# A hybrid diffusion step: the second chunk's operand forms made between products, and the squares of the group norm made during the attention

## Chip, core and metric

The kernel runs as one program on one core of a Trainium2 chip. The metric is the device time of one execution in microseconds, taken as the median of several runs. Engines are named as in the profile: TensorE (PE), VectorE (DVE), ScalarE (ACT), GpSimd (POOL) and SyncE (SP, which issues nearly all DMAs). In the trace each engine runs its own instructions in one fixed order, so one that waits holds up those behind it.

## What is computed

The reference is one inference step of a two-layer trunk over 1024 latent and 256 context tokens of width 1024. Cut to what matters here, a layer is:

```python
y = jnp.concatenate([rmsnorm(y_hy, gg[:D_HYENA]),
                     rmsnorm(y_sc, gg[D_HYENA:D_HYENA + D_SCONV]),
                     rmsnorm(y_at, gg[D_HYENA + D_SCONV:])], axis=-1)
x = x + g1 * (y @ P['w_out'][l])

h2 = rmsnorm(x, P['g_norm2'][l]) * (1 + sc2) + sh2
ff = (jax.nn.silu(h2 @ P['w_ff_gate'][l]) * (h2 @ P['w_ff_up'][l])) @ P['w_ff_down'][l]
x = x + g2 * ff
```

Three mixers (a long convolution, a short one and an attention of 8 heads) give `y_hy` (256 channels), `y_sc` (256) and `y_at` (512). Each group has its own RMS norm, and one output projection follows. Then comes a gated feed-forward part of inner width 2816. All is float32.

## The kernel before

**Layout.** Channels lie on the 128 partitions and tokens along the free dimension. Tokens are cut into three chunks (`CH`): 0 and 1 are 512 latent tokens each, 2 is the 256 context tokens. A float32 product is made of three matmuls: each operand is split into a high part (a cast on ScalarE) and a low part (a subtraction on VectorE or GpSimd), and high·high, high·low and low·high are added up in PSUM (`mm3`, `mma`; matmul lines L354 and L362). Such a pair of high and low is called a form.

**Order.** The program is written once; a planner then sets the order on each engine, mostly that of the program, with later work put into gaps that it foresees. A second planner lays out the memory called the arena: a buffer may lie where an earlier one was, and then its first write waits for the earlier one's last reader. `self.al` takes a buffer from the arena; rings (`t5`, `hb`, `sw`, `raw`) are small sets of slots used in turn.

**Attention and norm of groups.** `mla` runs blocks (head, bi), bi 0 being the context, 1 and 2 the latent halves, ending with (6,0) (6,1) (7,0) (7,1) (6,2) (7,2). In a block each turn makes one tile of scores (PE, tile `st`), its exponentials (ACT, L1292, tiles `pt`), a running sum of them (POOL, L1295) and every other turn the products with the values (PE, L1277). Some turns after a block of an odd head, `divide` adds up the sums (PE, L1316), takes the reciprocal (DVE, L1325) and multiplies (POOL, L1326). After the division of head 7, `tail` calls `group_norm` for chunk 2, 0 or 1. This loads seven stored tiles of that chunk (`yd`, two DMAs, L1445 and L1446; the eighth tile is the last head pair's result), squares all eight (ACT, L500 and L503) and adds the squares in groups of 2, 2 and 4 (DVE, L504). `bcast_rstd` sums over partitions (PE, L526), takes the inverse root in eleven small steps on DVE (L376 to L383), makes a diagonal (DVE, L535) and broadcasts it (PE, L539). Then each tile is scaled (DVE, L1457) and split (ACT L1459, DVE or POOL L1460). The output projection of chunk 2 runs as a filler inside the attention with one pair of weight buffers (`zo`); that of chunks 0 and 1 comes behind it with weights in `zw`. Its results are added to x (DVE, L1479).

**Gate and up.** The 22 tiles of the inner width are taken in 11 sets j of two, each for `w_gate` (g) and `w_up` (u). The latent product of a set is a 2×2 by 2×2 block product with seven products in place of eight: A is the weight (two inner tiles, two halves of the 1024 inputs), B the tokens (two halves of the inputs, chunks 0 and 1). Weight forms beside the blocks are S1 = A21+A22, S2 = S1−A11, S3 = A11−A21, S4 = A12−S2 (sums on POOL, L1521; high part ACT L1528, low part DVE L1529, in a ring `zq` of five). Token forms are 11 and 21 (chunk 0), 22 (chunk 1's lower half), T1 = B12−B11, T2 = B22−T1, T3 = B22−B12 and T4, which is B21−T2 up to sign. The products are 11·11, 12·21, S2·T2, S1·T1, S3·T3, S4·22 and 22·T4, 12 matmuls of 512 columns each; the context tokens have two plain products of 24 matmuls of 256 columns each (`context`, `contexts`). A set is thus 2 × 132 = 264 matmuls.

Only in set 0 must the token forms of chunk 1 still be made. `rest` does that: `norm2(1)` scales chunk 1 (DVE, L579, eight operations) and `forms_rest` makes the forms, group by group: T2 (POOL L621, DVE L622, cast L614 and subtraction L615, DVE L625), then T1 (L614, L615) with T3's sums (DVE L630), T3's splits, 22 (`shifted`, ACT L594, DVE L595), T4's splits. In the program all of it stands before set 0's first product:

```python
            if j == 0:
                need(0, "g")
                rest()
                first(0, "g")
                first(0, "u")
                for w in "gu":
                    contexts(0, w)
                    free(0, w, "22")
                second(0, "g")
                second(0, "u")
```

`need` fills the free slots of `zq` with weight forms in the order of the list `order`; `first` makes 11·11, one context product and 12·21, `contexts` the other context product, `second` the other five. Results go through `result` (PSUM read by DVE at L1576, L1581, L1585, L1615 and L1623; POOL L1582 multiplies gate and up) into slots of the ring `hb` and from there to memory.

Of the kernel before, what the change touches and what calls it, by code (L numbers as in the profile page):

```python
# [17 lines left out]
P = 128  # L18
# [217 lines left out]
class K:  # L236
# [365 lines left out]
    def forms_rest(self, l, u1, u2):  # L602

        nc = self.nc
        v, gp = nc.vector, nc.gpsimd
        sh = self.mod[l].v(2)[:, 24:32, 0]
        sm = self.small.alloc(4)
        d = sm.f[:, 0:4]
        v.tensor_tensor(out=d, in0=sh[:, 4:8], in1=sh[:, 0:4], op=ALU.subtract)
        F = {n: [None] * 4 for n in ("22", "T1", "T2", "T3", "T4")}  # L610
# [25 lines left out]
        for k in range(4):  # L636
            split("T4", k, u1[4 + k], gp)
        sm.free()
        return F

# [687 lines left out]
    def mla(self, l, tail):  # L1328
# [51 lines left out]
        def divide(head, bi):  # L1380
# [4 lines left out]
            if head == NH - 1:  # L1385
                tail((2, 0, 1)[bi], yats[NG - 1])
# [3 lines left out]
        turn, pend = 0, []  # L1390
        for head, bi in order:
# [48 lines left out]
    def group_norm(self, l, ci, yat):  # L1440
# [5 lines left out]
        nc.sync.dma_start(yv[:, 4:7, :], self.yd[l][:, 4:7, s:s + n])  # L1446
        src = [yv[:, k, :] for k in range(7)] + [yat.f[:, s:s + n]]
        hi, lo = [self.ar(n) for _ in range(KD)], [self.ar(n) for _ in range(KD)]
        groups = ((0, 2), (2, 4), (4, 8))
        accs = [(self.sumsq(src[a:b], n), 1.0 / (P * (b - a))) for a, b in groups]  # L1450
# [43 lines left out]
    def gate_up(self, l, cx, F, rest, extra, ahead):  # L1494
# [8 lines left out]
        order += [(0, w, n) for w in "gu" for n in ("S2", "S1", "S3", "22", "S4")]  # L1503
# [20 lines left out]
        def prepare():  # L1524
# [10 lines left out]
            if n == names[-1]:  # L1535
# [65 lines left out]
        def contexts(j, w):  # L1601
# [3 lines left out]
            result(w, "c", state[w]["E"])  # L1605

        def second(j, w):
# [16 lines left out]
            if j:  # L1624
                contexts(j, w)
# [13 lines left out]

        load(0, "g")  # L1640
        load(0, "u")
        for j in range(NF // 2):
            state["hid"] = {}
            if j == 0:
                need(0, "g")
                rest()
# [5 lines left out]
                second(0, "g")  # L1652
                second(0, "u")
# [76 lines left out]
    def run(self):  # L1730
# [60 lines left out]
        for l in range(DEPTH):  # L1791
# [6 lines left out]
            def tail(n, yat):  # L1798
                y[n] = self.group_norm(l, n, yat)
# [77 lines left out]
            self.close_rings("sw", "hb")  # L1877
# [171 lines left out]
```

## Time and profile before

| | us |
|---|---|
| median of 3 runs | 3706.76 |
| lowest, highest | 3701.41, 3712.45 |
| the profiled execution | 3703.83 |
| its span, first to last instruction | 3701.8 |
| busy in it: PE, DVE, ACT, POOL | 3435.0, 2337.1, 1245.1, 1440.2 |

The profile is of one execution. Its span is 2 us shorter than that execution's own time, and this lies 2.9 us under the median of the runs. Layer 0's gate and up starts near 1040 us, layer 1's near 2808 us; the ends of the two attentions lie around 800 to 940 and 2590 to 2720. In rows of a timeline a number in square brackets is the time that the engine stood idle before the instruction, with what ended that wait.

### The profile page before, as it was taken

What the parts mean: (1) busy time and instruction counts of PE and PEld (TensorE: products, weight loads), DVE (VectorE), ACT (ScalarE), POOL (GpSimd) and SP (SyncE); (2) the same over time, 40 slices, a digit from 0 to 9 for tenths busy, and PEclk for the clock granted to TensorE, in tenths of its full rate; (3) what the DMA queues carried; (4) which work ended last, traced back from release to release, by engine and by line L of the source; (5) the groups of instructions that cost most, each with busy time, mean ns of one, the idle gap of its engine ahead of it and who ended that gap; (6) DMA issues with size and microseconds to landing.
All of it is one profiled execution on the core that took longest, in us unless ns stands there. A gap on an engine that the chain in (4) does not pass through costs nothing.

```text
span 3701.8 us, 45689 instructions
## 1 busy us (share of the span) xinstructions
PE 3435.0 (93%) x17264; PEld 2705.9 (73%) x17264; DVE 2337.1 (63%) x3478; ACT 1245.1 (34%) x2245; POOL 1440.2 (39%) x1097
## 2 busy tenths in 40 slices
PE   7799889997879999999998988999897999999999
PEld 4488865655758888888886886655575888888888
DVE  4657577765476777546667757777658433435666
ACT  3522345544332222221114224555433322222110
POOL 3402346664443333332223223666645323223221
PEclk9899989999989999999999999999898999999999
DMA  7611100013423434342212210000451222214221
GB/s 275 241 60 61 42 10 11 19 39 128 145 65 113 134 123 125 114 154 85 96 58 74 65 47 14 4 11 19 134 165 55 83 69 69 71 61 154 97 77 69
DMA packets 118888, 317.87 MB, mean 86 GB/s; under 512 B 11371, under 2 KB 33387, under 8 KB 112652
## 3 DMA queue, kind: packets, MB, share of 16 engines
q1 hardware_dynamic: 118668, 314.96, 25.7%
q8 instruction: 135, 2.21, 0.3%
q14 instruction: 85, 0.70, 0.1%
HBM read 247.22 MB, written 67.70 MB: 85 GB/s over the span
## 4 chain that ended last, share of the span: by engine, by line
PE 76%; DVE 13%; issue 2%; ACT 2%; POOL 1%; DMA 1%; SPq 0%; DVEq 0%; POOLq 0%; ACTq 0%
PE pb L354 18%; PE pb L362 17%; PE pa L354 14%; PE pa L362 11%; PE st L354 6%; PE y L1277 4%; PE pa L1219 2%; DVE arena L852 1%; DVE arena L853 1%; PE pa L539 1%; PE pa L1238 1%; DVE arena L381 1%; PE pa L1231 1%; PE pa L1221 1%; DVE arena L383 1%
## 5 line engine op out<-in xcount | busy, mean ns | idle before, releaser
L354 PE MATMUL pb<-operands,zw 128*128 128x512 f32 (+1 forms) x2520 | 513.0, 361 | 5.7 <-DVE zw L345 3.0
L354 PEld LDWEIGHTS pb<-operands,zw 128*128 128x128 f32 x2520 | 427.1, 190 | 79.2 <-DVE zw L345 4.9
L362 PE MATMUL pb<-operands,zq 128*128 128x512 f32 (+1 forms) x2467 | 472.5, 348 | 5.5 <-DVE zq L1529 5.5
L1521 POOL TENSOR_TENSOR arena<-arena 128x512 f32<-128x512 f32 x176 | 262.1, 1491 | 523.3 <-DVE zq L1529 506.4
L1528 ACT CAST zq<-arena 128x512 fp32r<-128x512 f32 x356 | 220.8, 621 | 670.0 <-PE pb L362 428.4
L362 PEld LDWEIGHTS pb<-operands,zq 128*128 128x128 f32 x2467 | 391.7, 191 | 70.0 <-DVE zq L1529 6.9
L1529 DVE TENSOR_TENSOR zq<-arena,zq 128x512 fp32r<-128x512 f32 x356 | 288.7, 816 | 181.8 <-ACT zq L1528 177.6
L1295 POOL TENSOR_TENSOR arena<-pt,arena 128x512 f32<-128x512 f32 x256 | 334.7, 1307 | 93.7 <-ACT pt L1292 80.8
L354 PE MATMUL pa<-operands,zw 128*128 128x512 f32 (+1 forms) x1704 | 359.8, 368 | 1.1 <-DVE arena L558 0.6
L354 PEld LDWEIGHTS pa<-operands,zw 128*128 128x128 f32 x1704 | 296.2, 192 | 57.6 <-issue 3.6
L354 PE MATMUL st<-operands 97*128 97x512 f32 (+1 forms) x1056 | 321.0, 409 | 11.1 <-ACT pt L1292 11.1
L362 PE MATMUL pa<-operands,zq 128*128 128x256 f32 (+1 forms) x1801 | 320.8, 334 | 4.2 <-DVE zq L1529 4.2
L362 PEld LDWEIGHTS pa<-operands,zq 128*128 128x128 f32 x1801 | 272.5, 190 | 43.4 <-DVE zq L1529 4.9
L1708 DVE SCALAR_TENSOR_TENSOR arena<-pb,arena 128x512 f32<-128x512 f32 (+1 forms) x330 | 216.4, 661 | 115.4 <-PE pb L354 115.4
L1292 ACT ACTIVATE pt<-st 128x512 f32<-128x512 f32 (+1 forms) x352 | 202.4, 578 | 224.0 <-PE st L354 208.9
L354 PEld LDWEIGHTS st<-operands 97*128 97x128 f32 x1056 | 189.8, 196 | 116.0 <-issue 73.1
L344 ACT CAST zw<-arena 128x1024 fp32r<-128x1024 f32 x102 | 106.5, 1047 | 445.6 <-PE pb L354 374.4
L1277 PE MATMUL y<-pt,kv 128*64 128x512 f32 (+1 forms) x704 | 192.0, 616 | 0.0
L1220 DVE TENSOR_REDUCE arena<-pa 128x1 f32<-128x512 f32 x256 | 168.1, 686 | 34.8 <-PE pa L1219 30.7
L1708 DVE SCALAR_TENSOR_TENSOR arena<-pa,arena 128x512 f32<-128x512 f32 (+1 forms) x198 | 130.9, 661 | 92.8 <-PE pa L354 92.3
L362 PE MATMUL pb<-zf,zq 128*128 128x512 f32 x661 | 175.4, 403 | 10.5 <-DVE arena L1615 10.5
L354 PE MATMUL pb<-ze,zw 128*128 128x512 f32 (+1 forms) x900 | 182.4, 357 | 0.0
(279 smaller groups left out, 5576.6 us busy)
## 6 DMA issues: line engine op xcount, KB each, us to landing
hd<-arena SPq DMA_DIRECT2D x110, 256.0 KB, 2.1
zm<-in_w_modk SPq DMA_DIRECT2D x24, 1024.0 KB, 6.1
arena<-in_w_out SPq DMA_DIRECT2D x48, 512.0 KB, 3.6
arena<-in_w_mod SPq DMA_DIRECT2D x48, 512.0 KB, 3.5
arena<-in_w_g SPq DMA_DIRECT2D x44, 512.0 KB, 3.6
arena<-in_w_u SPq DMA_DIRECT2D x44, 512.0 KB, 3.6
arena<-in_w_dn SPq DMA_DIRECT2D x44, 512.0 KB, 3.8
arena<-hd SPq DMA_DIRECT2D x12, 1280.0 KB, 5.5
```

The source lines that it names most:

```text
L344: nc.scalar.copy(hi.r, raw.f)
L354: self.nc.tensor.matmul(out, a, b, start=(j == 0), stop=(j == n - 1))
L362: self.nc.tensor.matmul(out, a, b, start=(j == 0 and not add), stop=(j == n - 1), skip_group_check=add)
L1219: nc.tensor.matmul(p, q, kh[:96, 512 * c:512 * c + 512], start=True, stop=True)
L1220: v.reduce_max(out=mx[:, t, c:c + 1], in_=p, axis=AX.X)
L1277: ins = nc.tensor.matmul(y[64 * e:64 * e + 64, :n], G["kv"][:, kt0 + k + e, h, 0:64], pts[k + e].f[:, :n], start=(k == 0), stop=(k == nkt ...
L1292: ex = nc.scalar.activation(pt.f[:, :n], st[:, :n], AF.Exp)
L1295: (v if k in KDV else gp).tensor_tensor(out=acc.f[:, :n], in0=pt.f[:, :n], in1=(acc if k > 1 else pts[0]).f[:, :n], op=ALU.add)
L1521: gp.tensor_tensor(out=S[n].f, in0=a, in1=b, op=op)
L1528: nc.scalar.copy(f.r[:, 0:512], src)
L1529: v.tensor_tensor(out=f.r[:, 512:1024], in0=src, in1=f.f[:, 0:512], op=ALU.subtract)
L1708: nc.vector.scalar_tensor_tensor(out=xx, in0=p[:, :n], scalar=g2[:, m, q:q + 1], in1=xx, op0=ALU.mult, op1=ALU.add)
```

## The change

`forms_rest` becomes a generator that stops after each group of forms: T2, then T1, T3 (sums and splits together), 22, T4. Two of T2's four low parts (k = 0 and 2) go from GpSimd to VectorE. The new function `third` replaces `second` for set 0: it takes gate and up together through each product and lets the next group of forms be made behind it. The list of weight forms for set 0 runs in the same pairs, with S4 before 22. The context result c is written later. The ring `hb` has nine slots in place of eight, eight of them cut from the tiles of chunk 0, which therefore are freed at the end of the stage.

`group_norm` is split. `group_sums` allocates the place for the seven stored tiles, loads them, squares them and adds them up (ScalarE and GpSimd, in three buffers of the arena in place of slots of `t5`). It is called before blocks (7,0) and (7,1) for chunks 2 and 0, and in the first turn of block (7,2) for chunk 1. `group_norm` then squares the eighth tile alone and adds it on VectorE.

```diff
-    def forms_rest(self, l, u1, u2):
+    def forms_rest(self, l, u1, u2, F):
...
-            split("T2", k, t2.f, gp)
+            split("T2", k, t2.f, gp if k % 2 else v)
             v.scalar_tensor_tensor(out=u1[4 + k], in0=u1[4 + k], scalar=sh[:, 4 + k:5 + k], in1=t2.f, op0=ALU.add,
                                    op1=ALU.subtract)
             t2.free()
+        yield
         for k in range(4):
             split("T1", k, u1[k], v)
+        yield
+        for k in range(4):
             v.scalar_tensor_tensor(out=u2[k], in0=u2[4 + k], scalar=d[:, k:k + 1], in1=u2[k], op0=ALU.add,
                                    op1=ALU.subtract)
-        for k in range(4):
             split("T3", k, u2[k], gp)
+        yield
         for k in range(4):
             F["22"][k] = self.shifted(l, 4 + k, u2[4 + k])
+        sm.free()
+        yield
         for k in range(4):
             split("T4", k, u1[4 + k], gp)
-        sm.free()
-        return F
+        yield
...
+            if head == NH - 1 and bi < 2:
+                sums[bi] = self.group_sums(l, (2, 0)[bi])
...
+                if (head, bi, k) == (NH - 1, 2, 0):
+                    sums[bi] = self.group_sums(l, 1)
...
-    def group_norm(self, l, ci, yat):
+    def group_sums(self, l, ci):
+
         nc = self.nc
         s, n = CH[ci]
         yr = self.al(7 * n)
...
+        accs = []
+        for a, b in ((0, 2), (2, 4), (4, 7)):
+            acc = self.al(n)
+            nc.scalar.activation(acc.f, yv[:, a, :], AF.Square)
+            for k in range(a + 1, b):
+                q = self.t5(n)
+                nc.scalar.activation(q.f, yv[:, k, :], AF.Square)
+                nc.gpsimd.tensor_tensor(out=acc.f, in0=acc.f, in1=q.f, op=ALU.add)
+                q.free()
+            accs.append(acc)
+        return yr, yv, accs
+
+    def group_norm(self, l, ci, yat, early):
...
+        q = self.t5(n)
+        nc.scalar.activation(q.f, src[7], AF.Square)
+        nc.vector.tensor_tensor(out=accs[2].f, in0=accs[2].f, in1=q.f, op=ALU.add)
...
-        order += [(0, w, n) for w in "gu" for n in ("S2", "S1", "S3", "22", "S4")]
+        order += [(0, w, n) for n in ("S2", "S1", "S3", "S4", "22") for w in "gu"]
...
-            result(w, "c", state[w]["E"])
+            if j:
+                result(w, "c", state[w]["E"])
...
+        def third(more):
+
+            for w in "gu":
+                st = state[w]
+                st["Y"], st["a"] = self.ps(), self.t5()
+                (f,) = need(0, w, "S2")
+                self.mma(st["Y"], ops(f, F["T2"]), False)
+                free(0, w, "S2")
+                v.tensor_tensor(out=st["a"].f, in0=st["Y"], in1=st["p1"].f, op=ALU.add)
+            next(more)
+            for w in "gu":
+                result(w, "c", state[w]["E"])
+            for w in "gu":
+                st = state[w]
+                st["Z"] = self.ps()
+                (f,) = need(0, w, "S1")
+                self.mma(st["Z"], ops(f, F["T1"]), False)
+                free(0, w, "S1")
+            next(more)
...
             if j == 0:
                 need(0, "g")
-                rest()
+                more = rest()
+                next(more)
                 first(0, "g")
                 first(0, "u")
                 for w in "gu":
                     contexts(0, w)
                     free(0, w, "22")
-                second(0, "g")
-                second(0, "u")
+                third(more)
...
             def rest():
                 norm2(1)
-                F.update(self.forms_rest(l, h2[0], h2[1]))
-                x[0].free()
+                self.open_rings(hb0=("f", 512, 1))
+                hb0 = self.rings["hb0"]
+                self.rings["hb"] = Ring(hb0.bufs + Fixed(x[0].f, 4096).cut(512), 512)
+                more = self.forms_rest(l, h2[0], h2[1], F)
+                next(more)
+                yield
+                for _ in more:
+                    yield
                 x[1].free()
-                self.open_rings(hb=("f", 512, 8))
+                yield
```

The part of `third` left out goes on in the same way: S3·T3 and result 22, the next group; S4·22 and result 12, the next group; 22·T4 and result 21.

## Rows read from the trace of the kernel before

**Rows 1.** The page, part 1: busy time, share of the span, instructions of each engine.

```profile
PE 3435.0 (93%) x17264; PEld 2705.9 (73%) x17264; DVE 2337.1 (63%) x3478; ACT 1245.1 (34%) x2245; POOL 1440.2 (39%) x1097
```

**Rows 2.** Waits of PE: line waited for, us in total, times, longest.

```profile
PE pa L362 <- ACT zq L1528: 24.3, 4, 8.9
...
PE pa L526 <- DVE arena L504: 20.5, 9, 6.8
```

**Rows 3.** Windows, L362 alone: PE and PEld busy (matmuls), granted clock, DMA share, GB/s.

```profile
1039.80:1115.60 75.80, 57.00 (x263) 46.09 (x263) 0.84 0.24 77
2808.20:2884.40 76.20, 56.99 (x264) 46.05 (x265) 0.84 0.20 63
...
2900.00:2960.00 60.00, 60.00 (x318) 51.12 (x318) 1.00 0.21 67
```

**Rows 4.** Timeline of PE in layer 0, start of gate and up.

```profile
1064.58 0.40 PE L362 MATMUL pa<-operands,zq 128*128 128x256 f32 x2
...
1083.66 5.06 PE L362 MATMUL pa<-operands,zq 128*128 128x256 f32 x22 [4.15 <-DVE zq L1529]
```

**Rows 5.** Timelines of ACT (first row) and DVE in the same stretch.

```profile
1054.94 0.61 ACT L1528 CAST zq<-arena 128x512 fp32r<-128x512 f32 x1
...
1051.63 5.35 DVE L579 SCALAR_TENSOR_TENSOR arena<-arena,pa 128x512 f32<-128x512 f32 x8 [1.15 <-PE pa L539]
1056.90 2.01 DVE L622 SCALAR_TENSOR_TENSOR arena<-arena 128x512 f32<-128x512 f32 x2
...
1068.63 1.75 DVE L630 SCALAR_TENSOR_TENSOR arena<-arena 128x512 f32<-128x512 f32 x1
...
1082.93 1.88 DVE L1529 TENSOR_TENSOR zq<-arena,zq 128x512 fp32r<-128x512 f32 x3
```

**Rows 6.** POOL's timeline there; L1529's durations in ns, least, median, most.

```profile
1069.80 3.38 POOL L615 TENSOR_TENSOR operands<-arena,operands 128x512 fp32r<-128x512 f32 x2
...
L1529 DVE TENSOR_TENSOR zq<-arena,zq x356: 674/684/1804, 1040.7 to 3376.2; 128x512 fp32r<-128x512 f32 x178
```

**Rows 7.** Timeline of PE in layer 0, end of the attention.

```profile
868.77 1.05 PE L526 MATMUL pa<-arena 128*128 128x1 f32 x8 [2.91 <-DVE arena L504]
...
909.38 5.63 PE L354 MATMUL pb<-operands,zw 128*128 128x512 f32 x24
921.84 1.87 PE L526 MATMUL pa<-arena 128*128 128x1 f32 x8 [6.83 <-DVE arena L504]
...
933.35 5.46 PE L539 MATMUL pa<-arena 128*128 128x512 f32 x6 [3.40 <-DVE arena L535]
```

**Rows 8.** Chain that ended last, two pieces; SP's timeline, the load before.

```profile
913.54 1.30 POOL arena L1326
914.85 5.03 DMA arena<-yd
...
882.01 0.38 SPq L1446 DMA_DIRECT2D arena<-yd  x1
```

**Rows 9.** Timeline of DVE: first root step and first scaling of chunk 1, layer 0.

```profile
930.19 0.17 DVE L376 TENSOR_SCALAR arena<-arena 128x12 int32<-128x12 int32 x1
...
936.04 2.72 DVE L1457 SCALAR_TENSOR_TENSOR arena<-arena,pa 128x512 f32<-128x512 f32 x4
```

**Rows 10.** Timeline of PE in layer 1: first and last of three waits for L504.

```profile
2608.01 1.01 PE L526 MATMUL pa<-arena 128*128 128x1 f32 x4 [2.36 <-DVE arena L504]
...
2700.68 1.05 PE L526 MATMUL pa<-arena 128*128 128x1 f32 x8 [1.21 <-DVE arena L504]
```

**Rows 11.** Window with PE, PEld, DVE, ACT, POOL busy; a wait of ACT; L1295's durations.

```profile
820.00:840.00 20.00, 17.01 (x57) 8.31 (x57) 15.33 (x31) 9.43 (x21) 12.73 (x13) 0.83 0.17 58
...
ACT pt L1292 <- POOL arena L1295: 8.0, 7, 1.3
...
L1295 POOL TENSOR_TENSOR arena<-pt,pt x48: 721/1279/1712, 491.9 to 2644.9; 128x512 f32<-128x512 f32 x32, 128x256 f32<-128x256 f32 x16
```

More of the change, by code (lines that the diff above doesn't have):

```diff
@@ L609, in forms_rest @@
         v.tensor_tensor(out=d, in0=sh[:, 4:8], in1=sh[:, 0:4], op=ALU.subtract)
-        F = {n: [None] * 4 for n in ("22", "T1", "T2", "T3", "T4")}
+        F.update({n: [None] * 4 for n in ("22", "T1", "T2", "T3", "T4")})
         def split(name, k, t, e):
@@ L1385, in divide @@
             if head == NH - 1:
-                tail((2, 0, 1)[bi], yats[NG - 1])
+                tail((2, 0, 1)[bi], yats[NG - 1], sums.pop(bi))
         order = [(head, bi) for head in range(NH - 2) for bi in range(3)]
         order += [(NH - 2, 0), (NH - 2, 1), (NH - 1, 0), (NH - 1, 1), (NH - 2, 2), (NH - 1, 2)]
-        turn, pend = 0, []
+        turn, pend, sums = 0, [], {}
         for head, bi in order:
@@ L1446, in group_norm @@
         nc.sync.dma_start(yv[:, 4:7, :], self.yd[l][:, 4:7, s:s + n])
+        accs = []
[10 more added lines that the diff above has]
+    def group_norm(self, l, ci, yat, early):
+        nc = self.nc
+        s, n = CH[ci]
+        yr, yv, accs = early
         src = [yv[:, k, :] for k in range(7)] + [yat.f[:, s:s + n]]
+        q = self.t5(n)
+        nc.scalar.activation(q.f, src[7], AF.Square)
+        nc.vector.tensor_tensor(out=accs[2].f, in0=accs[2].f, in1=q.f, op=ALU.add)
+        q.free()
         hi, lo = [self.ar(n) for _ in range(KD)], [self.ar(n) for _ in range(KD)]
         groups = ((0, 2), (2, 4), (4, 8))
-        accs = [(self.sumsq(src[a:b], n), 1.0 / (P * (b - a))) for a, b in groups]
+        accs = [(acc, 1.0 / (P * (b - a))) for acc, (a, b) in zip(accs, groups)]
         rs = self.bcast_rstd(accs, n)
@@ L1534, in prepare @@
                     S[m].free()
-            if n == names[-1]:
+            if not any(t[:2] == (j, w) for t in todo):
                 for r in fs:
@@ L1638, in second @@
             p1.free()
+        def third(more):
[16 more added lines that the diff above has]
+            next(more)
+            for w in "gu":
+                st = state[w]
+                (f,) = need(0, w, "S3")
+                self.mma(st["Y"], ops(f, F["T3"]), True)
+                free(0, w, "S3")
+                b = self.t5()
+                v.tensor_tensor(out=b.f, in0=st["Y"], in1=st["p1"].f, op=ALU.add)
+                result(w, "22", st["Z"], b.f)
+                b.free()
+            next(more)
+            for w in "gu":
+                st = state[w]
+                (f,) = need(0, w, "S4")
+                self.mma(st["Z"], ops(f, F["22"]), True)
+                free(0, w, "S4")
+                result(w, "12", st["Z"], st["a"].f)
+                st["a"].free()
+            next(more)
+            for w in "gu":
+                st = state[w]
+                (f,) = need(0, w, "22")
+                self.mma(st["Y"], ops(f, F["T4"]), True)
+                free(0, w, "22")
+                result(w, "21", st["Y"], st["p1"].f)
+                st["p1"].free()
+            for _ in more:
+                pass
         load(0, "g")
@@ L1645, in gate_up @@
                 need(0, "g")
-                rest()
+                more = rest()
+                next(more)
                 first(0, "g")
@@ L1796, in run, with tail @@
             acc = {}
-            def tail(n, yat):
-                y[n] = self.group_norm(l, n, yat)
+            def tail(n, yat, early):
+                y[n] = self.group_norm(l, n, yat, early)
                 if n == 2:
@@ L1845, in rest @@
                 norm2(1)
-                F.update(self.forms_rest(l, h2[0], h2[1]))
-                x[0].free()
+                self.open_rings(hb0=("f", 512, 1))
+                hb0 = self.rings["hb0"]
+                self.rings["hb"] = Ring(hb0.bufs + Fixed(x[0].f, 4096).cut(512), 512)
+                more = self.forms_rest(l, h2[0], h2[1], F)
+                next(more)
+                yield
+                for _ in more:
+                    yield
                 x[1].free()
-                self.open_rings(hb=("f", 512, 8))
+                yield
             extra = iter(())
@@ L1876, in run @@
                     b.free()
-            self.close_rings("sw", "hb")
+            self.rings.pop("hb")
+            self.close_rings("sw", "hb0")
+            x[0].free()
             for part in "ab":
```

3 lines of the change are left out of this document (1 added, 2 removed).

## The prediction

> **What bounds the kernel now.** I read the page first: TensorE is busy for 3435 us, 93% of the span [rows 1]. An engine that full leaves two ways to a gain, its own idle time and the time at which its clock is low, so the second view was the list of waits for TensorE alone. The two groups in it that this change can reach are the matmuls of the first gate/up set, which waited 24.3 us for ScalarE's casts of weight forms, and the small sums of the norm of groups (L526), which waited 20.5 us for VectorE's additions L504 [rows 2]. Then I counted matmuls by stretch. The 264 matmuls of set 0 take 75.8 us in layer 0 and 76.2 us in layer 1; later sets run 318 in 60 us, so 264 would take 49.8 us [rows 3]. Each layer loses 26 us there, at a mean granted clock of 0.84 where it is 1.00 later [rows 3]. That is the pool of the first part.
>
> Where they go is seen in the timeline. Two matmuls into the second context product TensorE stops at 1064.98; up to 1083.66 it waits three times (16.4 us together; the last wait is shown), does four matmuls between, and then runs 22 narrow matmuls in 5.06 us [rows 4]. What it lacks is the low half of the weight form u21: ScalarE cast the high half at 1054.94, and VectorE subtracts at 1082.93, because 20 operations on forms of the second chunk (T2's eight, T1's and T3's four each, 22's four), begun at 1056.90, stand before it in VectorE's order [rows 5]. They would take 14 us at VectorE's usual 0.68 us [rows 6]; they took 26, because beside GpSimd one takes 1.75 us (L630 at 1068.63, [rows 5]) while two of GpSimd's take 3.38 us [rows 6]. GpSimd has 12 subtractions in that time (four each for T2, T3 and T4), so VectorE loses about 1.0 us per GpSimd instruction.
>
> At the end of the attention of layer 0 TensorE stops at 915.0 and waits four times, the first wait ended at 921.84 and the last at 933.35 (12.7 us together); the six broadcast matmuls behind that take 5.46 us [rows 7]. The chain of waits tells why: the last division ends at 914.84, only then does the load of chunk 1's tiles from memory go out, and it takes 5.03 us [rows 8]. The squares, additions and the scaling follow; the scaling L1457 begins at 936.04 [rows 9].
>
> **The change, part by part.** The sum is made against the profiled execution, 3703.8 us (span 3701.8); the median of the three runs is 3706.8, so 2.9 is added at the end.
>
> *Forms, per layer.* T2 stays ahead of the first products, with two of its four subtractions moved from GpSimd (1.69 us each) to VectorE; T1, T3, 22 and T4 move behind the weight forms of the products before them. In set 0 VectorE has, from 1051.6 on, 8 scalings (5.35 us, [rows 5]), 32 operations on two SBUF tiles (22 on forms of the tokens, 10 on weight forms) and 12 that read PSUM. The 44 at 0.68 us [rows 6] are 30 us, so 35.3 us alone. Beside it GpSimd has 24 instructions (4 differences, 10 subtractions, 7 weight sums, 3 products). If none collided VectorE would end at 1087, and TensorE's own 49.8 us plus 1.5 for the norm would bound the set at 1091; if each costs 1.0 us, the end is 1051.6 + 35.3 + 24 = 1111. Before it was 1115.6. So the two ends are a gain of 24 and of 4. Following the order by hand: T2's ten VectorE operations at about 1.2 us end at 1068, so u21 is ready at 1069 and TensorE waits some 4 us where it waited 16. Each later form has the two products before it to be made in, 24 matmuls or 5.6 us (as the 24 of [rows 7]): T1 is in time, T3's GpSimd halves end about level with the need (2 to 4 us lost), 22 and T4 have slack. With a clock loss of 1 to 2 us that gives 1101 to 1103. I take 13 us per layer, nearer to the collided end (4) than to the free one (24) because 12 of 12 collided before: 26 for both. The other moves (weight forms in pairs g, u; result c later; hidden slots laid over chunk 0's tiles; one slot more) issue nothing new and no DMA. They cost nothing as long as a slot's readers are done: result c goes over the first source of T1, read one product earlier. If that cover fails, the price is one wait for a GpSimd subtraction, 1.7 us; a gain is not to be had from them, since no result waited for a slot.
>
> The Trainium skill's page "SBUF — State Buffer" (section "SBUF: two separate sides") says that VectorE with two SBUF inputs and GpSimd take one port pair as an exclusive lock for a whole instruction, the loser standing still. The trace agrees with the blocking, not with the whole length: about 1.0 us is lost per instruction [rows 5, 6], not GpSimd's 1.3 to 1.7. By the page's rule with 1.3 us for each of the 24 the set would end at 1118 and this part would bring nothing.
>
> *Sums, per layer.* Added and removed work balances: 21 squares stay on ScalarE and are only earlier; 12 additions go from VectorE to GpSimd (8 wide, 4 narrow); the six loads are the same, issued earlier on SP; behind each division one square, one addition and eight sums per group remain. Layer 0: the wait of 2.9 us for chunk 0's additions goes [rows 7]. For chunk 1 the chain from 914.84 to the scaling was 21.2 us; what is left is 0.6 (square), 0.7 (addition), 1.1 (sums), 2.5 (square root, 11 steps of 0.2, the first at 930.19 before [rows 9]) and about 2 (diagonal and broadcast), 7 us. Of TensorE's 12.7 us some 3 remain, since out-projection matmuls of chunk 0 can fill but the root can't be shortened; with 2 us of clock given back that is 12. Layer 1 had its chunk 1 loaded in time: the three waits that end behind L504, the first of 2.36 us and the last of 1.21, are all that goes, 5.8 [rows 10]. Together 20.7.
>
> Against this stands GpSimd: 13.3 us more per layer in a stretch where it is also the adder of the softmax sums. The widths are those of its other additions, 1279 ns and 721 ns [rows 11]. No row shows that load. The lower end is 0, since GpSimd was busy 12.7 of 20 us there (VectorE, relieved of the additions, does not end this stretch, so there is no gain below 0); the upper is all 13.3, if ScalarE's exponentials wait for freed slots, as they did for 8.0 us in the whole kernel [rows 11]. Nearer to the first: 1.5 per layer, 3. The loads are moved past the weight loads on SP. Before, chunk 1's load of three tiles went out at 882.01 [rows 8], so SP stood for a place in memory there already. So I count nothing more, and it is landed by 890, ahead of 914.
>
> Sum: 26 + 20.7 − 3 = 44, so 3660 profiled and **3663 us** as a median.
>
> **The rivals.** *Collisions eat the forms.* All 24 GpSimd instructions collide at 1.0 us: 4 per layer instead of 13, total 26, 3681 us. For it: 12 of 12 before. Against: the moved GpSimd work now falls between VectorE's reads of PSUM too. By the Trainium skill's rule named above (the loser blocked for the whole instruction) this part would come to 0, and the time to 3689. 17%.
>
> *The second chunk's load is still late.* Memory is laid out by a planner; if it again puts chunk 1's tiles over something that the last division frees, the 12 us in layer 0 stay: 3675 us. For it: that is what the plan before did [rows 8]. Against: the tiles now live across that division, so they can't lie over what it frees. 12%.
>
> *No real change.* The planner of engine orders puts the forms ahead anyway, or the wait turns up one product later and behind the out-projection: 5 us, 3702. For it: VectorE was busy 26 us on end. Against: the products that can run in that time are there, and only order kept them back. 8%.
>
> *Slower.* Seven squares of chunk 1 stand in ScalarE's order ahead of the last block's exponentials while their load, behind SP's head, waits for chunk 0's scaling. If they are placed from 853 on, ScalarE stands until 882 plus 5 of load: 34 us without scores, in both layers 68; less the 44, 3731. It decides from 28 us per layer on (56 against 44, over 0.3%). For it: orders are fixed, and a load did wait until 882.01 [rows 8]. Against: the planner sees the same wait. 8%.
>
> **Numbers.** Forecast 55%, with a range of its own of 3643 to 3678 (forms 8 to 18 per layer, sums 12 to 24). About 0.3%, or 11 us, is what a measurement of this kernel can tell from no change. Faster: 55 + 17 + 12 = 84%; same 8%; slower 8%. The range goes from 3638 (forms at 22 per layer, sums at 24) to 3690 (forms at 4 per layer, sums near 9), so that it takes in both lesser gains and leaves out the last two rivals and a little at the low end.
>
> **What would show it.** Right: set 0's 264 matmuls take 60 to 66 us; DVE's u21 subtraction stands within 14 us of ScalarE's cast; no load of stored tiles starts after the last division; TensorE's wait for L504 is gone and the scaling of chunk 1 follows the division by about 7 us. Wrong: VectorE or GpSimd fully busy through all of set 0 with TensorE waiting on T3 or T4; ScalarE idle behind a square that waits for a load in the last block; exponentials waiting for GpSimd far above 8 us.

## The result and the profile after

The changed kernel took **3671.13 us** (median of 4 runs, 3669.24 to 3673.27), the kernel before 3709.26 in the same comparison: a ratio of 0.9911, 95% interval 0.9896 to 0.9927, faster by 0.9%. The forecast was 3663 (3638 to 3690). The profiled execution has a span of 3671.3 us, 30.5 less than before. TensorE's and VectorE's work is about what it was, GpSimd has 20 instructions more (the additions that came, less two of T2 per layer). The page, part 1, of the changed kernel, beside [rows 1]:

```profile
PE 3428.4 (93%) x17264; PEld 2700.9 (74%) x17264; DVE 2331.8 (64%) x3458; ACT 1244.2 (34%) x2245; POOL 1462.0 (40%) x1117
```

Waits of TensorE (line waited for, us in total, times, longest), beside [rows 2]:

```profile
PE pa L539 <- DVE arena L535: 50.6, 13, 11.9
...
PE pa L539 <- issue: 9.8, 2, 6.4
...
PE pa L1242 <- DVE operands L1211: 9.2, 2, 4.6
...
PE pa L362 <- POOL zf L615: 3.9, 5, 1.1
PE pa L362 <- DVE zq L1558: 3.4, 1, 3.4
...
PE pa L526 <- POOL arena L1463: 2.3, 2, 1.6
...
PE pa L526 <- DVE arena L1475: 1.5, 3, 1.1
...
PE pa L526 <- DVE arena L504: 1.2, 1, 1.2
```

Both targets are gone: the 24.3 us for ScalarE's casts of weight forms are not among the waits, and of the 20.5 for L504 1.2 is left; L526 waits 3.8 us for what took its place (L1463, L1475). New are 9.8 us in front of the broadcasts L539 (1.3 before), and some 4 us for T1 and 5 for T3 (L615 on VectorE and on GpSimd).

Set 0, the windows of L362 alone (busy of PE and PEld, granted clock, DMA share, GB/s), beside [rows 3]:

```profile
1024.00:1093.90 69.90, 59.16 (x264) 47.66 (x264) 0.90 0.23 80
2784.80:2853.60 68.80, 56.33 (x263) 44.67 (x263) 0.95 0.23 70
```

It takes 69.9 and 68.8 us, where it took 75.8 and 76.2, and I had forecast 60 to 66. In layer 0 no matmul of L362 ran for 10.7 us of it (18.8 before); they took 59.2 us, where 49.8 is the time at full clock. Some of these 9.4 us are the clock's, which was at its lower level (1.2 GHz) in three pieces, 13.6 us together. Their windows (all lines; PE, PEld, DVE, ACT and POOL busy):

```profile
1028.00:1034.80 6.80, 6.80 (x27) 6.22 (x27) 4.16 (x16) 1.21 (x2) 0.00 (x0) 0.50 0.00 0
1055.30:1058.70 3.40, 3.40 (x16) 3.25 (x15) 3.40 (x4) 1.14 (x2) 3.20 (x2) 0.50 0.00 0
...
1068.90:1072.30 3.40, 3.40 (x10) 2.63 (x9) 3.40 (x6) 1.56 (x3) 0.87 (x1) 0.51 0.72 208
```

The second and the third begin right behind stops of 3.4 and 2.0 us, seen in the timeline of PE, beside [rows 4]:

```profile
1054.03 4.20 PE L362 MATMUL pa<-operands,zq 128*128 128x256 f32 x22 [3.40 <-DVE zq L1558]
...
1068.30 0.74 PE L362 MATMUL pb<-zf,zq 128*128 128x512 f32 x2 [2.01 <-DVE zf L615]
...
1074.93 0.96 PE L362 MATMUL pa<-zf,zq 128*128 128x512 f32 x3 [0.62 <-POOL zf L615]
1076.62 0.96 PE L362 MATMUL pa<-zf,zq 128*128 128x512 f32 x3 [0.72 <-POOL zf L615]
1078.30 0.50 PE L362 MATMUL pa<-operands,zq 128*128 128x512 f32 x1 [0.72 <-POOL operands L615]
```

The wait for u21 is 3.4 us, T1 (DVE's L615) is 2.0 us late, and T3's low parts come from GpSimd one by one. The timelines of ScalarE (first row, u21's cast), VectorE and GpSimd tell why, beside [rows 5, 6]. ScalarE and VectorE:

```profile
1039.99 0.62 ACT L1557 CAST zq<-arena 128x512 fp32r<-128x512 f32 x1
...
1052.22 5.14 DVE L1558 TENSOR_TENSOR zq<-arena,zq 128x512 fp32r<-128x512 f32 x3
...
1060.18 1.77 DVE L615 TENSOR_TENSOR zf<-arena,zg 128x512 fp32r<-128x512 f32 x1
1061.88 1.78 DVE L615 TENSOR_TENSOR zf<-arena,zf 128x512 fp32r<-128x512 f32 x1
```

GpSimd:

```profile
1051.71 6.79 POOL L615 TENSOR_TENSOR operands<-arena,operands 128x512 fp32r<-128x512 f32 x4
1059.73 3.37 POOL L1550 TENSOR_TENSOR arena<-arena 128x512 f32<-128x512 f32 x2 [1.23 <-DVE zq L1558]
```

VectorE subtracts for u21 12.2 us behind the cast, after T2's ten operations. The planner put T4's four subtractions, last in the program, ahead of T1's. Beside them three of VectorE's took 5.14 us instead of 2.0; beside the weight sums L1550 two of T1's took 1.8 each.

At the end of the attention of layer 0 chunk 1's load goes out early, beside [rows 8]. The timeline of SyncE, and GpSimd's last division in it:

```profile
878.83 0.38 SPq L1454 DMA_DIRECT2D arena<-yd  x1
882.46 0.38 SPq L1455 DMA_DIRECT2D arena<-yd  x1
...
909.51 1.30 POOL L1330 TENSOR_TENSOR arena<-arena 128x512 f32<-128x512 f32 x1 [4.42 <-DVE arena L1329]
```

VectorE's timeline, from the addition behind the division (L1475) to the scaling (L1486), beside [rows 9]:

```profile
912.15 1.54 DVE L1475 TENSOR_TENSOR arena<-arena 128x512 f32<-128x512 f32 x1
...
921.97 1.41 DVE L1486 SCALAR_TENSOR_TENSOR arena<-arena,pa 128x512 f32<-128x512 f32 x2 [1.02 <-PE pa L539]
```

From the division's end (910.81) to the scaling are 11.2 us, where 21.2 were and 7 were forecast. The same sums for chunk 2 went the other way. The timeline of GpSimd, ScalarE and VectorE 90 us earlier, ahead of chunk 2's division (L1330) and in its square root:

```profile
819.56 1.55 POOL L1463 TENSOR_TENSOR arena<-arena 128x256 f32<-128x256 f32 x2
...
821.14 0.37 ACT L1306 COPY arena<-y 64x256 f32<-64x256 f32 x1 [2.42 <-POOL arena L1463]
...
823.65 0.75 POOL L1330 TENSOR_TENSOR arena<-arena 128x256 f32<-128x256 f32 x1
...
827.13 1.21 DVE L377 TENSOR_SCALAR arena<-arena 128x6 int32<-128x6 int32 x1
828.37 1.19 DVE L381 SCALAR_TENSOR_TENSOR arena<-arena 128x6 f32<-128x6 f32 x1
```

L1306 evicts the values of the last head's chunk 2. It stands behind seven early squares, and waits for a slot of `t5` that an addition of squares (L1463) still holds. The division needs it and so comes at 823.65, 15.2 us after the division before it; in the kernel before it was 8.8. Then the eleven steps of the square root took 8.2 us, since half of them met one of GpSimd's additions and took 1.1 to 1.2 us instead of 0.2 (3.3 us with one such step before), and TensorE stood still for 6.4 us.

The 30.5 us by stretches of the two profiled spans, from starts of instructions, the differences rounded from more digits (A is GpSimd's last division in the group of heads before the last one, at 808.05 before and 808.46 after in layer 0; the one of chunk 2 above is the next):

| stretch | before | after | difference |
|---|---|---|---|
| start to A of layer 0 | 808.1 | 808.5 | +0.4 |
| A to the start of gate and up, layer 0 | 231.8 | 215.6 | −16.2 |
| the first 420 matmuls of gate and up, layer 0 | 110.1 | 101.5 | −8.6 |
| from there to A of layer 1 | 1442.7 | 1446.9 | +4.2 |
| A to the start of gate and up, layer 1 | 215.6 | 212.3 | −3.3 |
| the first 420 matmuls, layer 1 | 105.6 | 98.6 | −7.1 |
| rest | 787.9 | 787.9 | +0.1 |

So the forms brought 15.7 where 26 were forecast, the stretches of the sums 19.5 where 17.7 were. Of the +4.2, 2.6 come from one wait near 2507 (for L1211: 4.6 us, 2.05 before), in a part that the diff doesn't touch; where the rest lies is open.

### The profile page after: what moved, and what is told of

The parts are those of the page before. It is cut to its first block, busy times and chain, and to the rows that moved or that the text cites. A ratio compares the mean times of both kernels' runs of the same rounds, so it can differ in the third digit from the quotient of the medians.

```text
span 3671.3 us, 45654 instructions
## 1 busy us (share of the span) xinstructions
PE 3428.4 (93%) x17264; PEld 2700.9 (74%) x17264; DVE 2331.8 (64%) x3458; ACT 1244.2 (34%) x2245; POOL 1462.0 (40%) x1117
## 4 chain that ended last, share of the span: by engine, by line
PE 78%; DVE 12%; ACT 2%; issue 2%; POOL 1%; DMA 1%; SPq 0%; DVEq 0%; ACTq 0%; POOLq 0%
PE pb L354 19%; PE pb L362 18%; PE pa L354 15%; PE pa L362 10%; PE st L354 5%; PE y L1281 4%; PE pa L1223 2%; PE pa L539 1%; DVE zq L1558 1%; DVE arena L856 1%; PE pa L1242 1%; DVE arena L857 1%; DVE arena L381 1%; PE pa L1225 1%; PE pa L1235 1%
## 5 line engine op out<-in xcount | busy, mean ns | idle before, releaser
L362 PE MATMUL pb<-operands,zq 128*128 128x512 f32 (+1 forms) x2466 | 473.2, 348 | 6.2 <-DVE zq L1558 5.1
L1550 POOL TENSOR_TENSOR arena<-arena 128x512 f32<-128x512 f32 x176 | 265.2, 1509 | 515.5 <-DVE zq L1558 494.2
L362 PEld LDWEIGHTS pb<-operands,zq 128*128 128x128 f32 x2466 | 391.8, 191 | 70.8 <-DVE zq L1558 6.0
L1558 DVE TENSOR_TENSOR zq<-arena,zq 128x512 fp32r<-128x512 f32 x356 | 301.6, 853 | 177.4 <-ACT zq L1557 173.1
L362 PE MATMUL pa<-operands,zq 128*128 128x256 f32 (+1 forms) x1802 | 319.9, 333 | 5.6 <-DVE zq L1558 3.4
L362 PEld LDWEIGHTS pa<-operands,zq 128*128 128x128 f32 x1802 | 272.1, 189 | 44.6 <-DVE zq L1558 3.6
L1296 ACT ACTIVATE pt<-st 128x512 f32<-128x512 f32 (+1 forms) x352 | 201.7, 578 | 215.1 <-PE st L354 200.1
L362 PE MATMUL pb<-zf,zq 128*128 128x512 f32 x660 | 174.1, 400 | 10.9 <-DVE arena L1645 8.8
```

Source lines behind the costliest of these rows:

```text
L362: self.nc.tensor.matmul(out, a, b, start=(j == 0 and not add), stop=(j == n - 1), skip_group_check=add)
L1296: ex = nc.scalar.activation(pt.f[:, :n], st[:, :n], AF.Exp)
L1550: gp.tensor_tensor(out=S[n].f, in0=a, in1=b, op=op)
L1558: v.tensor_tensor(out=f.r[:, 512:1024], in0=src, in1=f.f[:, 0:512], op=ALU.subtract)
```

## The experiments

All were timed in five rounds beside the kernel before (medians 3703.3, 3705.7 and 3708.6 us in the three groups of four). The changed kernel's own figure is 0.9911 [0.9896, 0.9927].

**1 and 2. Each half alone.** The first restores the old `group_norm` in the changed kernel, the second adds `group_sums` to the kernel before:

```diff
-                sums[bi] = self.group_sums(l, (2, 0)[bi])
...
-                    sums[bi] = self.group_sums(l, 1)
...
-    def group_norm(self, l, ci, yat, early):
+    def group_norm(self, l, ci, yat):
```

> The changed kernel with the norm of groups as it was before: only the change to the forms is left. Theory (read from the times at equal numbers of matmuls in the two traces): the forms bring 9 to 11 us per layer, the norm of groups 8 to 12 in both layers together, so this kernel takes 3684 to 3691, set 0 of layer 0 still takes about 70 us and chunk 1's scaling follows the last division by about 21 us again. Rival 1: the forms bring all of the gain and the early sums nothing, because GpSimd's additions take back what they give: 3669 to 3675. Rival 2: the forms bring less than 10 in all, what looked like their gain is carried over from the attention: 3697 or more.

> The kernel before with the early loads, squares and additions of the norm of groups, its forms untouched. Theory: 8 to 12 us below the kernel before, 3695 to 3701; layer 0 gains about 10, layer 1 nothing or loses up to 3. Rival 1 (GpSimd's additions take back all): 3706 to 3712. Rival 2 (forms and sums help one another, so the parts are worth less alone): the gains of this kernel and of the one with the forms alone add up to less than 30 of the 38 us.

Forms alone: 3684.49 us, 0.9944 [0.9931, 0.9958], about 21 us. Sums alone: 3695.72 us, 0.9982 [0.9971, 0.9994], about 7 (2 to 11). Together they give 27 of the 33 that the ratio of both gives. That is below the 30 of the second rival of run 2; with 4 to 6 us of uncertainty in each figure it neither shows nor excludes that the halves help one another. The first theory's total and its set 0 held, its last clause did not (17.0 us instead of 21, below). The second's range holds by the median, its 8 to 12 us only within the interval, and layer 1 gained 2.8 us in the profile where nothing or a loss was expected. The stretches show something that the totals hide:

| kernel | A to gate/up, layer 0 | layer 1 | set 0's 264, layer 0 | layer 1 |
|---|---|---|---|---|
| before | 231.8 | 215.6 | 76.2 | 76.2 |
| changed | 215.6 | 212.3 | 69.9 | 69.1 |
| forms alone | 215.5 | 218.3 | 69.8 | 69.4 |
| sums alone | 223.4 | 212.8 | 75.1 | 76.5 |

(Set 0 runs here from its first matmul to the first of set 1; the windows above that hold 263 of the 264 are shorter by as much.) The forms alone shorten layer 0's attention end by 16.3 us, though nothing of it is changed. SyncE's timeline of that kernel, in which these loads still stand behind the last division in the program (L1449 and L1450 are the former L1445 and L1446):

```profile
880.69 0.38 SPq L1449 DMA_DIRECT2D arena<-yd  x1
884.37 0.38 SPq L1450 DMA_DIRECT2D arena<-yd  x1
```

The loads go out some 30 us ahead of the division's end (913.4). Presumably the memory planner, given other lifetimes (chunk 0's tiles now last until gate and up ends), laid chunk 1's tiles where they need not wait for the division; no row shows the layout itself. The late load of [rows 8] was an accident of the old layout; either half of the change removes it (with the sums alone the loads go out at 882.0 and 885.7). The chain from division to scaling is 17.0 us in the kernel with the forms alone, 11.2 in the changed one, but chunk 0's division comes 47.0 us after A in the first and 52.8 in the second.

**3. The additions of squares on VectorE.**

```diff
-                nc.gpsimd.tensor_tensor(out=acc.f, in0=acc.f, in1=q.f, op=ALU.add)
+                nc.vector.tensor_tensor(out=acc.f, in0=acc.f, in1=q.f, op=ALU.add)
```

> The changed kernel with the early additions of squares on VectorE instead of GpSimd. Theory: GpSimd's additions slow the square-root steps of chunks 2 and 0 (8.2 and 6.1 us in layer 0 where they took 3.3 and 5.3) and stand before its softmax additions; on VectorE the roots go back to 3 to 5 us and the kernel gains 4 to 10 us: 3661 to 3667. Rival 1: the slow root is hidden behind scores and values, and only the order of the work counts: 3669 to 3673. Rival 2: VectorE's added 12 additions of about 0.7 us per layer stand in its order ahead of the divisions and the root themselves: 3675 to 3685.

3671.66 us, 0.9912 [0.9899, 0.9925]: the first rival's number, and the theory fell. The timeline of ScalarE and GpSimd shows what it had missed:

```profile
823.39 0.37 ACT L1306 COPY arena<-y 64x256 f32<-64x256 f32 x1 [1.73 <-DVE arena L1463]
...
825.75 1.19 POOL L1330 TENSOR_TENSOR arena<-arena 128x256 f32<-128x256 f32 x1
```

The division is as late as in the changed kernel (15.5 us after A), because the eviction L1306 still stands behind the squares and waits for a slot, now from VectorE's additions. The root stayed slow too (829.2 to 836.0), next to GpSimd's softmax additions. So the engine of the additions does not make the division late; the early squares and the slots which they share with the eviction became the next theory.

**4. T4 bound to come last.** ScalarE's casts of T3 are bound behind T1's last one, those of T4 behind T3's last.

```diff
-            nc.scalar.copy(hi.r, t)
+            ins = nc.scalar.copy(hi.r, t)
+            if name in ("T4", "T3"):
+                after(ins, {"T4": "T3", "T3": "T1"}[name])
+            if k == 3:
+                cast[name] = ins
```

> The changed kernel with T3's casts bound to come after T1's last one and T4's after T3's last one, so that T4 can no longer be made ahead of T1. Nothing is added or taken out. Theory: T4's four GpSimd subtractions, made first, slowed three VectorE subtractions of weight forms to 5.1 us and held back GpSimd's weight sums, for which ScalarE then waited; with T4 last, set 0 of layer 0 takes 62 to 65 us instead of 70, and the kernel 3657 to 3663. Rival: the sum of VectorE's and GpSimd's work in set 0 is the bound wherever T4 stands; its collisions only come later, TensorE waits for T3 or T4 instead, set 0 stays at 68 to 72 us and the kernel at 3668 to 3674.

3670.47 us, 0.9910 [0.9897, 0.9923]: the rival. TensorE's stop for T1 shrinks from 2.0 to 1.15 us, but T4 now meets 22's VectorE operations. The timeline of GpSimd, VectorE and TensorE (L625 is the former L615, L1615 L1605):

```profile
1076.24 6.78 POOL L625 TENSOR_TENSOR operands<-arena,operands 128x512 fp32r<-128x512 f32 x4
...
1078.45 3.44 DVE L595 SCALAR_TENSOR_TENSOR operands<-arena,operands 128x512 fp32r<-128x512 f32 x2
...
1084.22 7.41 PE L362 MATMUL pb<-operands,zq 128*128 128x512 f32 x24 [4.34 <-DVE arena L1615]
```

Set 0 took 71.5 us in layer 0 and 70.7 in layer 1 (69.9 and 69.1 in the changed kernel). Order alone moves the collisions, it doesn't remove them.

**5 and 10. Early sums for chunk 1 alone, and for chunks 2 and 0 alone.** Where `early` is None, `group_norm` calls `group_sums` itself. The cut shows run 5; run 10 sets the call for chunk 1 to None instead:

```diff
-                sums[bi] = self.group_sums(l, (2, 0)[bi])
+                sums[bi] = None
...
-        yr, yv, accs = early
+        yr, yv, accs = early or self.group_sums(l, ci)
```

> The changed kernel with the early loads, squares and additions for chunk 1 alone; chunks 2 and 0 make theirs behind their division, on GpSimd, with the new grouping. Theory: all that the early sums bring is chunk 1's in layer 0 (TensorE gained about 17 us there and lost about 7 in the stretch of chunks 2 and 0 before); without the early work of chunks 2 and 0 that loss goes, and the kernel takes 3663 to 3669. Rival 1: the work moved early costs no more there than where it stood: 3669 to 3673. Rival 2: the waits for chunk 2's and chunk 0's additions come back (4.5 us in layer 0, 2.4 and 2.2 in layer 1), and are longer on GpSimd than they were on VectorE: 3675 to 3683.

> The changed kernel with the early sums for chunks 2 and 0 alone; chunk 1's load, squares and additions stand behind the last division again, the additions on GpSimd. Theory: chunk 1's early sums bring all of the gain of that part (about 20 us), those of chunks 2 and 0 cost about 7 in a stretch where GpSimd adds the softmax sums: 3685 to 3695, slower than or level with the kernel that has the forms alone (3684). Rival: chunks 2 and 0 have a share in the gain: 3674 to 3681.

Chunk 1 alone: 3664.16 us, 0.9886 [0.9871, 0.9902]. Chunks 2 and 0 alone: 3686.55 us, 0.9948 [0.9935, 0.9962], level with the forms alone. Both theories held: all of the gain is chunk 1's. The size of what the early work for chunks 2 and 0 costs is rough: 9 us by the ratios of run 5 and the changed kernel, whose intervals overlap, under 2 by those of run 10 and the forms alone. The traces put it between: from A to gate and up, layer 0 takes 211.9 us in run 5 beside 215.6 in the changed kernel, and 221.8 in run 10 beside 215.5 with the forms alone, so 3.7 and 6.3 us; in layer 1 (209.9 beside 212.3, 217.0 beside 218.3) nothing clear. The timeline of ScalarE and GpSimd with chunk 1 alone:

```profile
809.54 0.37 ACT L1306 COPY arena<-y 64x256 f32<-64x256 f32 x1 [0.73 <-PE y L1281]
...
819.32 0.75 POOL L1330 TENSOR_TENSOR arena<-arena 128x256 f32<-128x256 f32 x1
```

Without the early squares of chunk 2 the eviction runs at A's own time, where it ran 12.7 us behind it, and the division stands 9.8 us after A. It is so in every kernel: with early squares of chunk 2, 15.2 to 19.5 us in both layers, without them 8.5 to 9.8.

**6, 7, 8. GpSimd's share of the forms.** All of T2's low parts on GpSimd again (6); those of T3 and T4 on VectorE (7); T2, T3, T4 and set 0's weight sums on VectorE (8). Of the cuts the first is run 6's, the next two are in both 7 and 8, the last is run 8's, which gives all of T2 to VectorE besides.

```diff
-            split("T2", k, t2.f, gp if k % 2 else v)
+            split("T2", k, t2.f, gp)
...
-            split("T3", k, u2[k], gp)
+            split("T3", k, u2[k], v)
...
-            split("T4", k, u1[4 + k], gp)
+            split("T4", k, u1[4 + k], v)
...
-                gp.tensor_tensor(out=S[n].f, in0=a, in1=b, op=op)
+                (gp if j else v).tensor_tensor(out=S[n].f, in0=a, in1=b, op=op)
```

> The changed kernel with all four low parts of T2 on GpSimd again, as before. Theory of collisions (one GpSimd instruction beside VectorE costs it about 1.0 us, whatever its length): two more GpSimd instructions of 1.7 us in the chain of T2, 3 to 4 us per layer in set 0, so 3676 to 3680. Rival: T2 is made while TensorE still has the first products to do, and its place on GpSimd costs nothing: 3669 to 3673.

> The changed kernel with the low parts of T3 and T4 on VectorE (eight subtractions per layer taken from GpSimd). Theory of collisions: VectorE gets 8 x 0.68 = 5.4 us more and loses 8 x 1.0 to 1.1 us less, and T3's chain of 1.7 us per low part becomes one of 0.68; set 0 of layer 0 takes 63 to 66 us instead of 69, and the kernel 3660 to 3666. Rival 1: VectorE's own work is the bound of set 0 and GpSimd a relief: set 0 takes 72 to 76 us, the kernel 3677 to 3685. Rival 2: neither: 3669 to 3673.

> The changed kernel with the low parts of T2, T3 and T4 and the eight weight sums of set 0 on VectorE: of GpSimd's work in set 0 only four differences and the products are left. Theory of collisions: 18 instructions of 0.68 us come to VectorE (12.2 us) and 18 collisions of 1.0 to 1.1 us go (18 to 20), and ScalarE no longer waits for GpSimd's weight sums (14.8 us in the changed kernel, both layers together); VectorE then sees no step of 1.7 us in set 0, which takes 59 to 64 us, and the kernel takes 3653 to 3664. Rival: with 60 operations VectorE is full from T2 to the end of set 0, TensorE waits for it as long as before or longer: set 0 at 70 us or more, the kernel at 3671 to 3685.

Run 6: 3677.44 us, 0.9929 [0.9915, 0.9942]. Run 7: 3661.95, 0.9879 [0.9862, 0.9895]. Run 8: 3664.12, 0.9889 [0.9873, 0.9904]. The theory of collisions gave the right number for 7 and missed by 0.1 us for 8. For 6 the number fits, but the interval overlaps the changed kernel's, and the trace does not show the 3 to 4 us per layer that were expected in set 0: it took 70.9 and 68.3 us, where the changed kernel took 69.9 and 69.1. So run 6 settles nothing. The windows of set 0 in layer 0, to within three matmuls of its end (length, then busy time and count of PE, PEld, DVE, ACT, POOL, granted clock, DMA share, GB/s) say how. The changed kernel:

```profile
1024.00:1093.20 69.20, 60.04 (x272) 48.69 (x271) 61.67 (x78) 29.92 (x50) 38.98 (x25) 0.90 0.22 76
```

Run 7, T3 and T4 on VectorE:

```profile
1032.70:1096.40 63.70, 57.40 (x273) 45.89 (x272) 58.79 (x86) 30.18 (x50) 27.43 (x18) 0.95 0.28 94
```

Run 8, all of it:

```profile
1025.30:1089.00 63.70, 57.67 (x274) 45.23 (x273) 57.70 (x91) 29.87 (x49) 17.50 (x12) 0.95 0.29 95
```

VectorE does 8 instructions more in run 7 (8 x 0.68 = 5.4 us) and is busy 2.9 us **less**: 8.3 us for the seven GpSimd instructions that left the window. In run 8 it does 13 more (8.8 us) and is busy 4.0 less, 12.8 us for 13. So by these windows one GpSimd instruction costs VectorE 1.0 to 1.2 us on average, more than the 0.68 that the same work costs on VectorE itself. A second count is lower: the time by which VectorE's instructions of set 0 exceed the shortest of their kind is 19.2 us in the changed kernel (26 GpSimd instructions), 12.8 in run 7 (18) and 7.4 in run 8 (12), which is 0.8 us for each that went (0.8 to 0.9 in layer 1).

Collisions are not the whole of run 7's gain, and no run separates it from a second cause: T3's low parts no longer come one by one from the slower engine. The timeline of TensorE in run 7, its stops for u21 and T3:

```profile
1061.72 2.85 PE L362 MATMUL pa<-operands,zq 128*128 128x256 f32 x22 [2.34 <-DVE zq L1558]
...
1078.33 2.13 PE L362 MATMUL pa<-zf,zq 128*128 128x512 f32 x8 [1.21 <-DVE zf L615]
```

TensorE's stops of over 0.5 us in set 0 fell from 9.2 to 5.5 us in layer 0, where the clock rose from 0.90 to 0.95 as well, and from 11.1 to 5.4 in layer 1, where the clock stayed at 0.95. Set 0 itself got 5.6 and 5.8 us shorter. T3's stops were 2.1 and 3.3 us, of which one of 1.2 and one of 1.1 are left; most of the rest came off u21 (3.4 to 2.3 in both layers) and T1 (2.0 to 1.0, and 2.4 to none).

Run 8 goes no further than run 7. VectorE is busy for 91% of set 0 in run 8, 92% in run 7 and 89% in the changed kernel. From 7 to 8 it gets five instructions more (3.4 us) and is busy 1.1 us less: 4.5 us for the six that left GpSimd, 0.75 each, hardly more than they cost on VectorE.

**9, 11, 12. Both cuts together.** Run 9 is chunk 1 alone (5) with T3 and T4 on VectorE (7), run 12 has T2 on VectorE too, run 11 is the changed kernel again.

> The changed kernel with both cuts that helped: early sums for chunk 1 alone, and the low parts of T3 and T4 on VectorE. Theory: the two lie in different stretches and add up: 7 us and 9 us below the changed kernel, 3654 to 3658. Rival: the gain of one was a faster start of the other's stretch (they overlap): 3660 to 3664.

> The changed kernel itself, unaltered, beside the others on this chip: 3668 to 3674 if its place does not depend on the call; the distances of the other runs are then read against it.

> The changed kernel with early sums for chunk 1 alone and the low parts of T2, T3 and T4 all on VectorE; GpSimd keeps the differences, the weight sums and the products. Theory of collisions: two more GpSimd instructions go from the chain of T2; putting two there cost about 6 us over both layers, so taking two away gives up to as much: 3650 to 3656. Rival: VectorE is full in set 0 by its own work by now, each instruction more costs it 0.7 us: level with the kernel that keeps T2 divided, 3654 to 3660.

Run 11: 3674.37 us, 0.9911 [0.9895, 0.9927], just over the expected 3674, with the same ratio as the first time. Run 9: 3655.87, 0.9860 [0.9845, 0.9874]. Run 12: **3650.96 us**, 0.9851 [0.9837, 0.9865], some 22 us below the changed kernel. The cuts of run 9 add up, as the theory had it. Run 12's number fits its theory, but the step from 9 to 12 lies inside the intervals, so what T2's part brings is not shown. Set 0 of layer 0 in run 12, same columns:

```profile
1021.50:1083.80 62.30, 57.05 (x274) 45.54 (x273) 56.56 (x88) 29.94 (x51) 23.89 (x16) 0.95 0.30 97
```

Run 11's profile has the same span as the first, 3671.3 us, but its layer 1 took 208.9 us from A to gate and up where the first took 212.3: 3 us of one stretch in a single profile are no finding.

## Why the prediction came out right

**Set 0, forecast 60 to 66 us, gain 13 per layer: mis-sized; 8.6 and 7.1.** The mechanism was right in the main. u21's wait fell to 3.4 us (4 forecast), its subtraction stands 12.2 us behind the cast (within 14, as forecast), and T3's halves cost 2.1 us in layer 0 (2 to 4 forecast) and 3.3 in layer 1. Two things failed. "T1 is in time" did not hold, it cost 2.0 and 2.4 us: the order by hand followed the program, while the planner put T4 first. Run 4 shows that the order alone was not the loss, since a stop of 4.3 us came in place of T1's. And "a clock loss of 1 to 2 us" was too small: the granted clock was 0.90 in layer 0 and 0.95 in layer 1, where 13.6 and 6.8 us stood at the lower level and so cost up to 6.8 and 3.4; with the slow pieces the matmuls of layer 0 took 59.2 us where full clock gives 49.8. With seven stops of 0.6 to 3.4 us in the stretch the clock was not at its upper level throughout, and the sum has to carry that. The sum has a slip besides: its terms end at 1098 to 1101 and not at 1101 to 1103, so that by them the gain would have been some 14 to 17 us, not 13.

The price per collision, 1.0 us, came out for those that occur: in set 0 of layer 0, 20 of VectorE's 79 instructions ran over, by 19 us together, beside 26 GpSimd instructions: most of these collided, not all. What I did not draw from the price is that the subtractions left on GpSimd cost about as much as they relieve, or more.

By the Trainium skill's page "SBUF — State Buffer" (section "SBUF: two separate sides"), the port pair is locked for a whole instruction, and the part, as the prediction worked it out, would have come to nothing. The runs agree with the blocking, but a hit costs about 1.0 us (19 us for 20), not GpSimd's 1.3 to 1.7; the forms gained 15.7 us.

**Sums, forecast 20.7 − 3 = 17.7: 19.5, of other parts.** "No load of stored tiles after the last division" and "the wait for L504 is gone" held. "Scaling about 7 us behind the division" measured 11.2: the addition took 1.5 us beside a GpSimd instruction instead of 0.7, the root 3.9 instead of 2.5 since two of VectorE's other operations were put between its steps, and diagonals and broadcast 3.0 instead of 2. TensorE still waited 3.6 us at L539 for the diagonals, where some 3 were to remain. But the 12 us of layer 0 were not the sums' own. The kernel with the forms alone has layer 0's stretch at 215.5 too: its load is early by layout. That this part's total came out near its forecast is luck.

**GpSimd's 13.3 us, priced 3 for both layers through exponentials: the wrong mechanism, and probably too low.** ScalarE's waits in the changed kernel, beside [rows 11]:

```profile
ACT arena L1306 <- POOL arena L1463: 5.4, 2, 3.0
ACT pt L1296 <- POOL arena L1299: 5.0, 4, 1.6
```

The exponentials (L1296) wait 5.0 us for GpSimd, less than the 8.0 before. The price is paid by the eviction L1306 behind the early squares, in slots of `t5`, and by a root of 8.2 us: chunk 2's division is 6.4 us later behind A in layer 0, 10.4 in layer 1. Runs 5 and 10 put the whole at under 2 to 9 us, their traces at 3.7 and 6.3 in layer 0. The rival on the slower side named a kin of it (squares in ScalarE's order ahead of what the last block needs) but in the wrong place: it was chunk 2's squares ahead of an eviction, not chunk 1's ahead of exponentials.

**The other rivals.** Collisions eating the forms' gain (3681, 4 us per layer) came true in part: 8.6 and 7.1 us lie about halfway between it and the forecast. One of the signs of being wrong showed too: VectorE was busy for 89% of set 0 while TensorE waited for T3. The late load (3675) did not happen, but the reason given was not needed for it: with the forms alone, where the tiles do not live across the division, the load is early as well. "Nothing for the other moves" can't be told apart from the total; no result waited for a slot of `hb`.

So the median came out 8 us over the forecast. In the profiled spans 44 was the sum and 30.5 the gain: the forms were 10.3 too high, the sums 1.8 too low, and some 5 us were lost elsewhere, most of it in work that the diff doesn't touch. (The bound 3643 of the forecast's own range does not follow from its terms either: forms at 18 and sums at 24 give 3647 or more.)

## What to carry to other kernels

A subtraction of two tiles given to GpSimd relieves a full VectorE only if its collision costs less than the operation itself; here it cost 0.8 to 1.2 us against 0.68, and the result came later from the slower engine, so the division of labour did not pay. Work that is done early "in gaps" takes slots and places in the queues from what was there: look for the short eviction or copy that now stands behind it, and do early only what the last chain needs. Where planners set order and memory, time each half alone, since a gain can come with either.

## Not expected of the hardware

A VectorE step of 6 columns, 0.17 us long, pays the same price as one of 512 columns when it meets a GpSimd instruction: it then takes 1.12 to 1.21 us, about 1.0 more, as 1.75 us in place of 0.68 does for the wide one. Where several short steps run in the time of one GpSimd instruction, only one is hit. It shows in the root of chunk 2, where six of eleven steps took over 1.1 us, and in that of chunk 1, where GpSimd was idle and none did (0.16 to 0.17 each).
